# Splitting streamed weights in halves of 1024 columns instead of quarters of 512

## The chip, the cores and the metric

The kernel runs on one core of a Trainium2 chip. The metric is the device time of one launch in microseconds, the median of several runs. An execution that the hardware profiler recorded gives the trace. TensorE (PE in the rows; PEld is its weight load) does the matmuls, VectorE (DVE) and ScalarE (ACT) work elementwise, SyncE (SP) issues the DMAs.

## What is computed

The reference is a decoder of two layers over one sequence of 256 tokens with 1024 channels, all in float32. Cut to what matters:

```
for each layer:
  h = modulate(rmsnorm(x), shift1, scale1)       # shift, scale, gate = silu(c) @ wada + bada
  p = h @ win                                    # one projection, 7200 columns, split in
      # A: latent attention (q rank 768, kv rank 256, rotary key 32), wuq, wkpe, wukv expand them
      # B: stick-breaking attention, 8 heads of 64
      # C: MoBA attention, 8 heads of 64, rope on a part of the head
      # three gates of 1024 columns (sigmoid)
  m = sum over A, B, C of sigmoid(gate) * (branch @ wo)
  x = x + gate1 * (m @ wout)
  h = modulate(rmsnorm(x), shift2, scale2)
  x = x + gate2 * (relu(h @ wff1)**2 @ wff2)
x = rmsnorm(x) * g
```

## The kernel before

The weights are streamed. A **job** is one weight tile `ws` of 128 partitions and up to 2048 float32 columns (1 MB), brought by a DMA on SP's queue (L154), three buffers deep. TensorE multiplies in a rounded format (fp32r), so a weight is split in a high part `wh` = round(`ws`), written by ScalarE (L177), and a low part `wl` = `ws` - `wh`, written by VectorE (L178); activations are split likewise (`split`, L233 to L235: `lh`, `ll` and so on). Each product is then three matmuls, `wh` by the high activation, `wh` by the low one, `wl` by the high one: `mm3` (L341 to L344), and L939 to L942 for the second feed-forward matrix. `wh` and `wl` have three buffers each.

The split of a job is cut into four pieces (`PIECES`), quarters of its columns: 512 for most jobs, 384 for the six of `wuq`, 256 for the two of `wkpe`. `run(i)` emits the matmul parts of job i and spreads over them the pieces of the jobs up to two further (`AHEAD`); `pump` between the parts runs generators of attention work. After the last piece of a job the DMA of a later one is issued (`fetch_to`). Beside these there are **raw** jobs: the matrix `wada` isn't multiplied on TensorE; VectorE multiplies and sums it in two halves of 1024 columns per job (`ada`, L242, then L247).

The prologue (L988 to L1081) is written in a fixed order (`manual_schedule`); its jobs carry a list of sources (several small DMAs), four of them are not split at all (`plain`), the other four in quarters. Elsewhere the compiler's scheduler orders each engine's instructions by its own estimate, from the order in the code and the dependencies. Each engine then executes its list in order.

Steps that the text behind speaks of:
- `sb_attn` (L488 to L517), stick-breaking attention: scores `z`, then on ScalarE abs, exp, ln (L497 to L499), on VectorE L500, the split in `lh` (L234) and `ll` (L235), matmuls `z` (L510) with these, exp to `a`, and `po` (L469).
- `rope` (L574 to L586): `raw` (ScalarE, L576, recorded at the helper's line L234) and `rl` (VectorE, L235) from a product in PSUM, a product with the cosine (L579), matmuls `rp` (L582, L583), a product with the sine (L585).
- `sigmoid` (L130 to L135): abs, exp, ln on ScalarE, L134 on VectorE, exp on ScalarE; used for the branch gates.
- `mla_v` (L747): matmuls `mvps` from `wukv`, in PSUM; `pt` (L560) are transpositions of softmax tiles; `s` (L521, L524) are the scores of latent attention, of `km` and `qm`; `qm` is written by copies on VectorE (L771).

Names of small tiles in rows can be those of a tile that shares the buffer (`csr` for a constant, `head` for another).

Of the kernel before, what the change touches and what calls it, by code (L numbers as in the profile page):

```python
# [11 lines left out]
F32 = mybir.dt.float32  # L12
# [3 lines left out]
AF = mybir.ActivationFunctionType  # L16
# [24 lines left out]
def trunk(ctx, tc, xT, heads, pos, signs, masks, gfin, wada, win, wkpe, wuq, wukv, wo, wout, wff1, wff2, out):  # L41
    nc = tc.nc
# [115 lines left out]
    def fetch_to(i):  # L158
        while state["dma"] <= min(i, len(jobs) - 1):
            for _ in fetch(state["dma"]):  # L160
                pass
            state["dma"] += 1

    def split_piece():
        i, pc = divmod(state["split"], PIECES)
        job = jobs[i]
        if job.raw:
            job.parts[pc](job.ws)
        elif job.plain:
            job.wh, job.wl = job.ws, None  # L170
        else:
            if pc == 0:
                job.wh = wpool.tile([128, 2048], F32R, name="wh", tag="wh", bufs=WB)
                job.wl = wpool.tile([128, 2048], F32R, name="wl", tag="wl", bufs=WB)
            n = job.f // PIECES
            a = slice(pc * n, pc * n + n)
            nc.scalar.activation(job.wh[:, a], job.ws[:, a], AF.Copy)  # L177
            nc.vector.tensor_sub(job.wl[:, a], job.ws[:, a], job.wh[:, a].bitcast(F32))  # L178
        state["split"] += 1
        if state["auto"] and pc == PIECES - 1:  # L180
            fetch_to(i + WS)

    def split_to(i, pc):
        while state["split"] < min(PIECES * i + pc, PIECES * len(jobs)):
            split_piece()
# [994 lines left out]
```

## Time and profile before

| | us |
|---|---|
| median of 3 runs | 937.77 (935.73 to 939.75) |
| profiled execution | 938.25 |
| its span | 936.5 |
| TensorE busy | 915.7 (98%) |
| VectorE busy | 730.5 (78%) |
| ScalarE busy | 599.1 (64%) |
| mean granted TensorE clock | 0.995 of full speed |

The span runs from the first to the last recorded instruction; the rest of the time lies around it. In rows of a timeline the first number is the start in us, the second the duration, "x7" means seven in a row, and the bracket at the end is the time that the engine was idle before, with what ended the wait. The duration of a matmul is longer than its distance to the next, since matmuls are pipelined.

### The profile page before, as it was taken

To read this page: it belongs to the slowest core of one execution; us is meant where nothing else is said; L and a number is where in the kernel's file an instruction comes from. 1 tells how busy PE (TensorE), PEld (TensorE's weight loads), DVE (VectorE), ACT (ScalarE), POOL (GpSimd) and SP (SyncE) were. 2 spreads that over 40 slices of the span, in tenths; PEclk is the share of its full clock that TensorE was granted. 3 is DMA by queue.
4 is the path that set the end of the run, shared out by engine and by line. 5 is a ranking of instruction groups with operands and counts; after the bars stand their busy time and mean duration, and the time that the engine had idled before them with its cause. 6 is when DMAs were issued, how large, how long until landed. Compare 5 with 4: busy or idle time off the path is not lost.

```text
span 936.5 us, 19142 instructions
## 1 busy us (share of the span) xinstructions
PE 915.7 (98%) x7771; PEld 889.6 (95%) x7772; DVE 730.5 (78%) x1414; ACT 599.1 (64%) x1251; POOL 9.6 (1%) x15
## 2 busy tenths in 40 slices
PE   7998999999999999999999999999999999999996
PEld 4998999899999999999999999989999999999995
DVE  6878788887799976767897978879787989554554
ACT  4277678867576874645576677886677677563641
POOL 0000000000000000000000000000000000000012
PEclk9999999999999999999999999999999999999998
DMA  9956564565657388677847554645666647755531
GB/s 339 386 205 231 185 225 159 214 235 196 245 225 270 140 310 305 236 270 266 324 174 274 222 203 155 229 169 210 240 221 228 212 150 284 256 181 190 186 121 45
DMA packets 32634, 208.77 MB, mean 223 GB/s; under 512 B 3745, under 2 KB 4130, under 8 KB 8994
## 3 DMA queue, kind: packets, MB, share of 16 engines
q1 hardware_dynamic: 32400, 207.35, 61.7%
q8 instruction: 61, 1.00, 0.4%
q0 software_dynamic: 144, 0.20, 0.1%
q14 instruction: 27, 0.22, 0.1%
q10 hardware_dynamic: 2, 0.00, 0.0%
HBM read 206.49 MB, written 1.05 MB: 222 GB/s over the span
## 4 chain that ended last, share of the span: by engine, by line
PE 84%; DVE 6%; DMA 6%; ACT 2%; issue 1%; SPq 0%; DVEq 0%; ACTq 0%
PE ps L342 17%; PE ps L343 16%; PE ps L344 16%; PE ff L939 5%; PE ff L942 5%; PE ff L940 5%; DMA ws<-win 5%; PE pre L364 4%; DVE wl L178 3%; PE po L469 1%; DMA ws<-wada 1%; PE vps L342 1%; PE vps L344 1%; PE vps L343 1%; PE s L524 1%; PE z L510 1%
## 5 line engine op out<-in xcount | busy, mean ns | idle before, releaser
L178 DVE TENSOR_TENSOR wl<-ws,wh 128x512 fp32r<-128x512 f32 (+1 forms) x592 | 378.7, 675 | 128.6 <-ACT wh L177 128.0
L177 ACT ACTIVATE wh<-ws 128x512 fp32r<-128x512 f32 (+1 forms) x592 | 336.8, 615 | 208.2 <-PE ps L343 97.3
L342 PE MATMUL ps<-act,wh 128*128 128x256 f32 x1120 | 312.0, 279 | 0.0
L344 PE MATMUL ps<-act,wl 128*128 128x256 f32 x1120 | 310.3, 277 | 0.0
L343 PE MATMUL ps<-act,wh 128*128 128x256 f32 x1120 | 310.1, 277 | 0.0
L342 PEld LDWEIGHTS ps<-act,wh 128*128 128x128 f32 x1120 | 210.4, 188 | 0.5 <-DVE wl L178 0.3
L344 PEld LDWEIGHTS ps<-act,wl 128*128 128x128 f32 x1120 | 210.9, 188 | 0.0
L343 PEld LDWEIGHTS ps<-act,wh 128*128 128x128 f32 x1120 | 210.4, 188 | 0.2
L939 PE MATMUL ff<-fh,wh 128*128 128x256 f32 x448 | 123.6, 276 | 0.0
L940 PE MATMUL ff<-fl,wh 128*128 128x256 f32 x448 | 123.6, 276 | 0.0
L942 PE MATMUL ff<-fh,wl 128*128 128x256 f32 x448 | 123.6, 276 | 0.0
L242 DVE SCALAR_TENSOR_TENSOR ws<-ws,cb 128x1024 f32<-128x1024 f32 x80 | 95.9, 1221 | 22.5 <-DMA ws<-wada 22.1
L939 PEld LDWEIGHTS ff<-fh,wh 128*128 128x128 f32 x448 | 84.1, 188 | 0.0
L940 PEld LDWEIGHTS ff<-fl,wh 128*128 128x128 f32 x448 | 84.1, 188 | 0.0
L942 PEld LDWEIGHTS ff<-fh,wl 128*128 128x128 f32 x448 | 84.1, 188 | 0.0
L544 ACT ACTIVATE e<-s,st 128x128 f32<-128x128 f32 (+1 forms) x64 | 26.0, 432 | 23.6 <-DVE st L539 23.6
L364 PE MATMUL pre<-xh,wh 128*128 128x258 f32 x96 | 28.3, 295 | 0.0
L364 PE MATMUL pre<-xh,wl 128*128 128x258 f32 x96 | 27.1, 283 | 0.0
L364 PE MATMUL pre<-xl,wh 128*128 128x258 f32 x96 | 27.1, 282 | 0.0
L342 PE MATMUL vps<-wh,act 128*128 128x256 f32 x96 | 26.9, 280 | 0.0
L343 PE MATMUL vps<-wl,act 128*128 128x256 f32 x96 | 26.7, 278 | 0.0
L344 PE MATMUL vps<-wh,act 128*128 128x256 f32 x96 | 26.7, 278 | 0.0
(259 smaller groups left out, 1738.6 us busy)
## 6 DMA issues: line engine op xcount, KB each, us to landing
ws<-wff SPq DMA_DIRECT2D x64, 1024.0 KB, 4.9
ws<-win SPq DMA_DIRECT2D x50, 1024.0 KB, 4.9
ws<-wada SPq DMA_DIRECT2D x40, 1024.0 KB, 4.9
ws<-wo SPq DMA_DIRECT2D x12, 1024.0 KB, 4.9
adaw<-wada SPq DMA_DIRECT2D x8, 1024.0 KB, 9.2
ws<-wout SPq DMA_DIRECT2D x8, 1024.0 KB, 4.9
ws<-win SPq DMA_DIRECT2D x24, 256.0 KB, 9.1
ws<-wuq SPq DMA_DIRECT2D x6, 768.0 KB, 4.3
```

Of the source, the lines that this page charges most:

```text
L177: nc.scalar.activation(job.wh[:, a], job.ws[:, a], AF.Copy)
L178: nc.vector.tensor_sub(job.wl[:, a], job.ws[:, a], job.wh[:, a].bitcast(F32))
L242: nc.vector.scalar_tensor_tensor(w, w, 1.0, cb, op0=OP.mult, op1=OP.mult, accum_out=mods[l][:, 2 * b + i:2 * b + i + 1])
L342: nc.tensor.matmul(o, wh, ah, start=first, stop=False)
L343: nc.tensor.matmul(o, wh, al, start=False, stop=False)
L344: nc.tensor.matmul(o, wl, ah, start=False, stop=last)
L364: nc.tensor.matmul(ps[:, i, 0:258], w[:, c:c + 128], a[:, k, :], start=k == 0 and n == 0, stop=k == KT - 1 and n == 2, skip_group_check=True)
L469: nc.tensor.matmul(po[64 * h:64 * h + 64, u, o:256], v[:, k, vc:vc + 64], pT[:, h, c:c + n], start=k == 0, stop=k == 1, tile_position=(0, ...
L544: nc.scalar.activation(e[:, h, a:b], s[:, h, a:b], AF.Exp, scale=scale, bias=st[:, 4 + c:5 + c], accum_out=st[:, 8 + c:9 + c])
L939: nc.tensor.matmul(o, wh[:, c0:c0 + 128], fh[:, k, :], start=st, stop=False, skip_group_check=True)
L940: nc.tensor.matmul(o, wh[:, c0:c0 + 128], fl[:, k, :], start=False, stop=False, skip_group_check=True)
L942: nc.tensor.matmul(o, wl[:, c0:c0 + 128], fh[:, k, :], start=False, stop=en, skip_group_check=True)
```

## The change

The piece counter stays as it is: four pieces per job, spread over the parts as before. But where a job's source is one matrix (not a list, so outside of the prologue), piece 0 now splits the first half of the columns at once, piece 2 the second half, and pieces 1 and 3 emit nothing. The halves have 1024 columns, 768 for `wuq` and 512 for `wkpe`.

```diff
             n = job.f // PIECES
-            a = slice(pc * n, pc * n + n)
-            nc.scalar.activation(job.wh[:, a], job.ws[:, a], AF.Copy)
-            nc.vector.tensor_sub(job.wl[:, a], job.ws[:, a], job.wh[:, a].bitcast(F32))
+            wide = 1 if isinstance(job.src, list) else 2
+            if pc % wide == 0:
+                a = slice(pc * n, (pc + wide) * n)
+                nc.scalar.activation(job.wh[:, a], job.ws[:, a], AF.Copy)
+                nc.vector.tensor_sub(job.wl[:, a], job.ws[:, a], job.wh[:, a].bitcast(F32))
```

Line numbers behind L178 are higher by 2 in the changed kernel. The order on SP and POOL is the same. On TensorE the same matmuls stand in nearly the same order; ScalarE and VectorE have fewer instructions, which the scheduler has placed anew.

VectorE, the first rope and the first stick-breaking block of layer 1 (about 65 to 78 us), before:

```order
L178 TENSOR_TENSOR wl<-ws,wh 128x512 x7
L247 TENSOR_TENSOR mod_90<-mod_90,head 128x2
L500 SCALAR_TENSOR_TENSOR l<-z,l 128x768
L235 TENSOR_TENSOR ll<-l,lh 128x768
L235 TENSOR_TENSOR rl<-ps,raw 128x512
L579 TENSOR_TENSOR mbqk<-ps,tab 128x512
L500 SCALAR_TENSOR_TENSOR l<-z,l 128x768
L178 TENSOR_TENSOR wl<-ws,wh 128x512 x3
L235 TENSOR_TENSOR ll<-l,lh 128x768
```

and now:

```order
L244 SCALAR_TENSOR_TENSOR ws,mod_90<-ws,cb 128x1024
L180 TENSOR_TENSOR wl<-ws,wh 128x1024 x3
L249 TENSOR_TENSOR mod_90<-mod_90,head 128x2
L502 SCALAR_TENSOR_TENSOR l<-z,l 128x768
L237 TENSOR_TENSOR ll<-l,lh 128x768
L180 TENSOR_TENSOR wl<-ws,wh 128x1024
L502 SCALAR_TENSOR_TENSOR l<-z,l 128x768
L237 TENSOR_TENSOR rl<-ps,raw 128x512
L581 TENSOR_TENSOR mbqk<-ps,tab 128x512
L237 TENSOR_TENSOR ll<-l,lh 128x768
```

A half of `wl` and the second `l` now stand ahead of `rl` and of the product with the cosine; before they stood behind it.

ScalarE at the same place, before:

```order
L498 ACTIVATE l<-l 128x768
L234 ACTIVATE raw<-ps 128x512
L499 ACTIVATE l<-l 128x768
L177 ACTIVATE wh<-ws 128x512 x4
L234 ACTIVATE lh<-l 128x768
```

and now:

```order
L500 ACTIVATE l<-l 128x768
L179 ACTIVATE wh<-ws 128x1024
L501 ACTIVATE l<-l 128x768
L236 ACTIVATE raw<-ps 128x512
L179 ACTIVATE wh<-ws 128x1024
L236 ACTIVATE lh<-l 128x768
```

`raw` has moved behind a half of `wh` and behind the logarithm of the second block.

VectorE ahead of the gate for which `mvps` waits in layer 1 (about 163 to 169 us), before:

```order
L235 TENSOR_TENSOR latl<-lt,lath 128x256 x2
L178 TENSOR_TENSOR wl<-ws,wh 128x384
L661 SCALAR_TENSOR_TENSOR lt<-lat,head,rr 128x256 x2
L178 TENSOR_TENSOR wl<-ws,wh 128x384 x2
L242 SCALAR_TENSOR_TENSOR ws,mod_90<-ws,cb 128x1024
L134 SCALAR_TENSOR_TENSOR gate<-ps,gate 128x512
```

and now:

```order
L237 TENSOR_TENSOR latl<-lt,lath 128x256
L180 TENSOR_TENSOR wl<-ws,wh 128x768
L663 SCALAR_TENSOR_TENSOR lt<-lat,head,rr 128x256 x2
L134 SCALAR_TENSOR_TENSOR gate<-ps,gate 128x512
```

The half of `ada` (L242, now L244) that stood directly ahead of the gate has gone to an earlier place; one of 768 columns stands there for three of 384.

## Rows read from the trace of the kernel before

**Rows 1.** The page, busy time of each engine: us, share, instructions.

```profile
PE 915.7 (98%) x7771; PEld 889.6 (95%) x7772; DVE 730.5 (78%) x1414; ACT 599.1 (64%) x1251; POOL 9.6 (1%) x15
```

**Rows 2.** Stretches: length, busy PE, PEld, DVE, ACT, POOL; granted clock, DMA share, GB/s.

```profile
400.00:425.00 25.00, 25.00 (x223) 25.00 (x222) 16.40 (x30) 13.66 (x27) 0.00 (x0) 1.00 0.77 277
...
617.00:623.00 6.00, 5.04 (x18) 4.10 (x19) 3.82 (x10) 4.79 (x12) 0.00 (x0) 0.72 0.55 186
```

**Rows 3.** Waits of TensorE: us in total, times, longest.

```profile
PE mvps L342 <- DVE gate L134: 4.3, 2, 2.2
...
PE rp L582 <- ACT wh L177: 1.0, 1, 1.0
PE z L510 <- DVE ll L235: 0.9, 1, 0.9
PE po L469 <- ACT wh L177: 0.6, 1, 0.6
...
PE s L521 <- DVE qm L771: 0.2, 1, 0.2
```

**Rows 4.** Groups by line and form: busy us, mean ns of one, idle before.

```profile
L178 DVE TENSOR_TENSOR wl<-ws,wh 128x512 fp32r<-128x512 f32 x552 | 360.2, 687 | 118.2 <-ACT wh L177 117.6
L177 ACT ACTIVATE wh<-ws 128x512 fp32r<-128x512 f32 x552 | 319.7, 625 | 203.9 <-PE ps L343 93.0 <-PE ff L940 46.3 <-PE xl L940 16.2
...
L242 DVE SCALAR_TENSOR_TENSOR ws<-ws,cb 128x1024 f32<-128x1024 f32 x80 | 95.9, 1221 | 22.5 <-DMA ws<-wada 22.1
...
L178 DVE TENSOR_TENSOR wl<-ws,wh 128x384 fp32r<-128x384 f32 x24 | 12.5, 554 | 6.5 <-ACT wh L177 6.5
L177 ACT ACTIVATE wh<-ws 128x384 fp32r<-128x384 f32 x24 | 11.4, 521 | 0.0
```

**Rows 5.** Timeline of VectorE, 65 to 78 us.

```profile
65.07 4.30 DVE L178 TENSOR_TENSOR wl<-ws,wh 128x512 fp32r<-128x512 f32 x7
...
69.36 0.95 DVE L500 SCALAR_TENSOR_TENSOR l<-z,l 128x768 f32<-128x768 f32 x1
...
73.29 0.69 DVE L235 TENSOR_TENSOR rl<-ps,raw 128x512 fp32r<-128x512 f32 x1 [1.11 <-ACT raw L234]
73.90 0.68 DVE L579 TENSOR_TENSOR mbqk<-ps,tab 128x512 f32<-128x512 f32 x1
...
77.16 0.95 DVE L235 TENSOR_TENSOR ll<-l,lh 128x768 fp32r<-128x768 f32 x1
```

**Rows 6.** Timeline of ScalarE, 72 to 76 us.

```profile
72.68 0.58 ACT L234 ACTIVATE raw<-ps 128x512 fp32r<-128x512 f32 x1
73.16 0.83 ACT L499 ACTIVATE l<-l 128x768 f32<-128x768 f32 x1
73.89 2.18 ACT L177 ACTIVATE wh<-ws 128x512 fp32r<-128x512 f32 x4
```

**Rows 7.** Timeline of TensorE, 73 to 79 us.

```profile
74.68 0.47 PE L582 MATMUL rp<-raw,csr 128*128 128x512 f32 x1 [1.02 <-ACT wh L177]
...
76.20 0.27 PE L510 MATMUL z<-ll,negs 128*128 128x128 f32 x1
...
78.17 0.44 PE L510 MATMUL z<-ll,csr 128*128 128x384 f32 x1 [0.87 <-DVE ll L235]
...
79.20 0.33 PE L342 MATMUL ps<-act,wh 128*128 128x256 f32 x1
```

**Rows 8.** Timeline of TensorE at the first `po`.

```profile
88.71 0.65 PE L469 MATMUL po<-a,v 128*64 128x256 f32 x4 [0.64 <-ACT wh L177]
```

**Rows 9.** Timeline of TensorE at `mvps`, layers 1 and 2.

```profile
169.31 0.47 PE L342 MATMUL mvps<-wh,lath 128*128 128x512 f32 x1 [2.20 <-DVE gate L134]
...
172.29 0.37 PE L342 MATMUL ps<-lath,wh 128*128 128x256 f32 x1
...
617.96 0.47 PE L342 MATMUL mvps<-wh,lath 128*128 128x512 f32 x1 [2.06 <-DVE gate L134]
...
622.28 0.56 PE L342 MATMUL ps<-lath,wh 128*128 128x256 f32 x1
```

## The prediction

> **What bounds the kernel now.** I read the busy shares first. TensorE is busy 915.7 us of a span of 936.5 us, VectorE 730.5 and ScalarE 599.1 us [rows 1]. So one engine fills the span, and the two that the change relieves are 78% and 64% busy. Next the table by stretch: in the feed-forward stretch from 400 to 425 us TensorE is busy for all 25.00 us at a granted clock of 1.00, 223 matmuls, which makes 112 ns each, while VectorE has work for 16.40 us and ScalarE for 13.66 us [rows 2]. There TensorE waits for nobody, and nothing that makes a split cheaper can shorten it.
>
> What is left for the change to win stands in the list of TensorE's waits [rows 3]: the two `mvps` matmuls that wait for VectorE's gate (4.3 us together), the first rope matmul `rp` (1.0), a `z` matmul that waits for `ll` (0.9), the first `po` (0.6) and a score `s` (0.2). The waits of the prologue are not in it, since its jobs keep their quarters. That is 7.0 us in all, 0.7% of the run.
>
> **The change: fewer, longer instructions.** The rows by form hold 552 + 24 splits at 512 and 384 columns on each of the two engines [rows 4], and 16 more at 256. The prologue keeps 16 of these 592 quarters; the other 576 become 288 halves, so 288 instructions go from each engine. What one saves follows from two sizes. On VectorE 512 columns take 687 ns and 384 take 554 [rows 4]: 133 ns for 128 columns, so 1024 should take 687 + 4 x 133 = 1219 ns; the 1024-column instruction that the kernel already has on VectorE, L242, takes 1221 [rows 4]. Neighbours overlap a little: seven splits took 4.30 us [rows 5], so one starts (4.30 - 0.69)/6 = 0.602 us after the other, 0.085 less than its duration. A half then occupies about 1.22 - 0.085 = 1.13 us against 1.204 for two quarters: 0.07 us saved. On ScalarE 512 take 625 ns and 384 take 521 [rows 4], so 1024 about 625 + 4 x 104 = 1041 ns; four took 2.18 us [rows 6], a distance of 0.52, so a half occupies about 0.94 us against 1.04: 0.10 us saved. Bounds for a half are no better than one quarter (0.60, 0.52) and no worse than two full durations (1.37, 1.25); I take the extrapolations, since L242 lies on the first. Over 288 halves that is 20 us of VectorE and 29 us of ScalarE.
>
> None of it is on the path by itself: in rows 2 both engines have a third of their time free. The cover is TensorE's queue of weights: with three buffers and a lead of two jobs a weight is split long before it is multiplied. If that cover were gone, the gain would be up to the waits of rows 3.
>
> The Trainium skill bears on this ("Perfetto Trace Analysis", section "Optimizing Scalar/DVE Operations"): larger operations help where the engine is saturated, and where Scalar or Vector aren't saturated but cause bubbles on other engines, breaking instructions up lets work complete sooner. By that rule the change goes the wrong way here and the time would come out above 937.8. The trace agrees with the rule's premise (rows 1 and 3: not saturated, small bubbles); it gives no price, and none of it enters the sum.
>
> **The change: what now stands in front of others.** Each engine takes its instructions in order, so what is queued behind a split now waits for up to another half: about 0.4 us more on ScalarE, 0.53 on VectorE. The issue order of the DMAs on SP's queue and the order on POOL's are the same. TensorE's order differs at six places, each a few neighbours. I walked every wait of TensorE with the new orders and these durations.
>
> Place A, the first rope of layer 1, 56 to 90 us. Before, ScalarE writes `raw` from 72.68, then L499, then four quarters from 73.89 [rows 6]; VectorE does `rl` at 73.29, the product L579 at 73.90 until 74.58 [rows 5], and `rp` starts behind it at 74.68 [rows 7]. In the new order one half of `wh` stands before L499, and `raw` behind both: 72.68 + 0.94 + 0.73 (the distance from L499 to what follows) = 74.35, and 0.2 later still, since one half of an ada job has moved between splits and delays the first L500 (before at 69.36 [rows 5]) a little. On VectorE a half of `wl` and the second L500 come ahead of `rl`: the half waits for its `wh` until about 73.9, ends near 75.1, then L500 0.87, `rl` 0.61 and L579 0.68. L579 ends at about 77.25 and `rp` starts at 77.35 instead of 74.68: 2.67 later. But much of this comes back. The second `z` block behind it waited for its `ll`, which started at 77.16 [rows 5], and so began its second matmul only at 78.17 [rows 7]. In the new order `lh` and `ll` are done at about 76.9 and 78.1, and TensorE gets there at 78.98 (`rp` and the first `z` block took 1.63 before: the last matmul of that block starts at 76.20 [rows 7], one matmul is 0.11). Nothing is waited for any more. From the second matmul of the block to the weight matmul behind it pass 79.20 - 78.17 = 1.03 [rows 7], about 0.15 more from the first, so that weight matmul starts at 80.16 instead of 79.20: +0.97. The same order comes once more before the first `po` (88.71 [rows 8]), where I get 89.75, which makes **+1.04 for the whole of A**. Its bounds: if ScalarE's halves cost two full quarters and nothing came back, 2.67 + 0.6 = +3.3; if the scheduler's rows meet earlier than I walked, no more than the waits there are lost, 1.0 + 0.9 + 0.6 = -2.5.
>
> Place B and its twin in layer 2, `mvps` at 169.31 and 617.96 [rows 9]. The gate's chain runs over both engines (abs, exp, ln on ScalarE, L134 on VectorE). In the new order one transposition `pt` has moved behind the wait, and the ada half that stood just ahead of L134 now stands earlier, with a half of 768 columns and two short steps in its place. An ada half is 1.22 us [rows 4], that half about 0.95 (687 + 2 x 133 ns), and its `wh` on ScalarE comes later by a quarter; I let them cancel, so the wait stays and the `pt` adds one matmul of 0.11 us, half of it hidden: **+0.05 each**. Bounds: the wait goes (-2.2 each [rows 3]), or grows by one half on each engine (+0.94).
>
> The scores `s` [rows 3] wait for copies that now stand behind a half of `wl`: **+0.2 each** in two layers, between -0.2 and +0.53. In the feed-forward stretches, the output products and the rest, the steps between a weight's split and its use have over 1 us to spare: 0, cover being the lead of two jobs.
>
> Sum: 1.04 + 2 x 0.05 + 2 x 0.2 = +1.5 us. The profiled execution took 938.25 us, 0.48 above the median of 937.77; 938.25 + 1.5 - 0.48 = 939.3 us for a median.
>
> **The clock.** It is a bound that the trace shows once. After `mvps` in layer 2 the granted clock fell: 0.72 in the stretch from 617 to 623 us [rows 2]; from the first `mvps` to the first `ps` it took 622.28 - 617.96 = 4.32 us, in layer 1, after a wait of the same length, 172.29 - 169.31 = 2.98 [rows 9]. Such a fall costs 1.34 us. Place A gets one idle stretch of 3.7 us where it had three short ones, and layer 1 may fall too. So the terms reach from -1.34 (the one in layer 2 goes) to +2.68.
>
> **The rivals.** First, *faster*: the freed time shortens the waits. The chains at A and `mvps` contain splits, and VectorE has less to do ahead of them. For it: 0.07 and 0.10 us per half, and an ada half less in front of the gate. Against it: a chain passes two or three halves at most, 0.3 us, and each half can block for longer than that. Its best is all of 7.0 us and the clock's 1.34: 937.8 - 8.3 = 929.4; half of it, 933.6, is no longer 0.5%.
>
> Second, *slower*: the doubled granularity bites at all attention steps. Place: the 12 ropes, the 8 blocks of `z` and the 24 gates, whose chains change engine two to four times and can meet a half on each. Price: 0.4 + 0.53 = 0.9 us per chain that TensorE waits for. Now TensorE waits at six places in all [rows 3]. If six more lose their spare microsecond, 6 x 0.9 = 5.4 us, and with the sum above 944.7 us. It decides where the chain's end has less than about 0.9 us before TensorE; in the walk the ropes and blocks behind place A have 1.5 us or more, which speaks against it. What speaks for it is that place A alone already loses 2.67 us at one step.
>
> Third, *nothing moves*: TensorE's wait at A is as in the trace and the chip hands out the same clock; 937.8. That the change doesn't do what it says is excluded: the orders have 288 splits fewer.
>
> **How the numbers follow.** Forecast, +0.5 to +3 us (938.3 to 940.8): 0.55. Nothing or a small gain, down to -4: 0.22, of which the most lies near 937.8. A loss from +3 to +4.7 (A at its bound, a clock fall): 0.12. Slower rival, over +4.7: 0.07. Faster rival, under -4.7: 0.04. A measurement of this kernel can tell about 0.5%, 4.7 us, from no change; all but the two rivals lie within it. The range leaves out the two rivals and the outer half of the small gains: 935.5 to 942.5.
>
> **What would show it.** Splits at 1024 columns of 1.22 us on VectorE and 1.04 on ScalarE, busy sums (of durations) down by 288 x (1.37 - 1.22) = 43 and 288 x (1.25 - 1.04) = 60 us. TensorE busy as before. `rp` preceded by one wait of over 3 us and no wait left in the `z` block behind it; the `mvps` waits at 2 to 2.4 us. I would be wrong on the mechanism if `mvps` waits fell under 1 us (the faster rival), or if new waits on `wl`, `raw` or `ll` appeared behind 100 us (the slower one).

## Result and profile after

The changed kernel takes 943.85 us (938.24 to 947.26, 17 runs) against 938.0 (933.92 to 942.85, 17 runs): a ratio of 1.0053, 95% interval 1.0036 to 1.0070. It is slower by 5 to 6 us; forecast were 939.3 and a range to 942.5. Its first profiled execution, 938.24 us, is the fastest of the 17 and does not contain the loss, so the same kernel was profiled three times more (`after_b`, `after_c`, `after_d` below).

The page of that first execution, the busy times (compare [rows 1]):

```profile
PE 917.0 (98%) x7771; PEld 890.5 (95%) x7772; DVE 709.8 (76%) x1126; ACT 576.6 (62%) x963; POOL 9.8 (1%) x15
```

288 instructions less on each engine, and 20.7 and 22.5 us less busy. The groups by line and form (busy us, mean ns of one, idle before), to be held against [rows 4]:

```profile
L180 DVE TENSOR_TENSOR wl<-ws,wh 128x1024 fp32r<-128x1024 f32 x272 | 327.8, 1222 | 135.0 <-ACT wh L179 132.7 <-PE ps L345 1.6
L179 ACT ACTIVATE wh<-ws 128x1024 fp32r<-128x1024 f32 x272 | 282.1, 1056 | 196.8 <-PE ps L345 95.0 <-PE ff L942 47.4 <-DMA ws<-wff 26.1
L180 DVE TENSOR_TENSOR wl<-ws,wh 128x768 fp32r<-128x768 f32 x12 | 11.3, 952 | 9.1 <-ACT wh L179 9.1
```

The extrapolated 1219, 1041 and 953 ns became 1222, 1056 and 952. (The busy sums fell by less than the sum of durations, since neighbours that overlap count once: the 20 and 29 us that the prediction had for occupied time are nearer than its 43 and 60.) TensorE's waits in the same execution (compare [rows 3]):

```profile
PE mvps L344 <- DVE gate L134: 2.6, 2, 1.4
PE s L523 <- DVE qm L773: 2.0, 2, 1.1
...
PE rp L584 <- ACT lh L236: 0.6, 1, 0.6
```

`mvps` waits less than in [rows 3], `s` much more.

### The profile page after: what moved, and what is told of

The parts are those of the page before. It is cut to its first block, busy times and chain, and to the rows that moved or that the text cites. A ratio compares the mean times of both kernels' runs of the same rounds, so it can differ in the third digit from the quotient of the medians.

```text
span 936.5 us, 18563 instructions
## 1 busy us (share of the span) xinstructions
PE 917.0 (98%) x7771; PEld 890.5 (95%) x7772; DVE 709.8 (76%) x1126; ACT 576.6 (62%) x963; POOL 9.8 (1%) x15
## 4 chain that ended last, share of the span: by engine, by line
PE 72%; DVE 10%; DMA 10%; ACT 5%; issue 2%; SPq 0%; DVEq 0%; ACTq 0%
PE ps L344 15%; PE ps L345 15%; PE ps L346 14%; DMA ws<-win 5%; DVE wl L180 4%; PE ff L942 4%; PE ff L941 4%; PE ff L944 4%; DMA ws<-wada 4%; PE pre L366 4%; DVE ws L244 2%; ACT wh L179 2%; PE po L471 1%; PE vps L344 1%; PE vps L346 1%
## 5 line engine op out<-in xcount | busy, mean ns | idle before, releaser
L180 DVE TENSOR_TENSOR wl<-ws,wh 128x1024 fp32r<-128x1024 f32 (+3 forms) x304 | 349.4, 1169 | 148.4 <-ACT wh L179 145.9
L179 ACT ACTIVATE wh<-ws 128x1024 fp32r<-128x1024 f32 (+3 forms) x304 | 301.2, 1013 | 207.5 <-PE ps L345 99.6
L244 DVE SCALAR_TENSOR_TENSOR ws<-ws,cb 128x1024 f32<-128x1024 f32 x80 | 96.2, 1219 | 28.8 <-DMA ws<-wada 28.8
```

What stands on the lines that cost most here:

```text
L244: nc.vector.scalar_tensor_tensor(w, w, 1.0, cb, op0=OP.mult, op1=OP.mult, accum_out=mods[l][:, 2 * b + i:2 * b + i + 1])
```

## The experiments

All ratios are to the kernel before on the same chip, with 95% intervals.

**Once more, and where.** `after_b` is the changed kernel again, `before_b` the one before. `halves_ff` and `halves_rest` split the change by a flag on the job:

```diff
-            wide = 1 if isinstance(job.src, list) else 2
+            wide = 2 if job.ff else 1                                        # halves_ff
+            wide = 1 if job.ff or isinstance(job.src, list) else 2           # halves_rest
```

> The changed kernel once more, for another profiled execution: the one at hand took 938.24 us, its median is 943.85, so it does not contain the 5.5 us. Theory C (clock): about 944 us, the granted clock near 0.991 instead of 0.996, with two to four stretches at a lower clock that the first profile lacks, TensorE's waits behind 56 us about 6 us in all as there. Theory W (waits, my slower rival): about 944 us at a clock near 0.995, with 5 us more of waits behind 56 us, on halves of wl, raw, ll or on a DMA of weights. Theory P (prologue): the 5 us stand before 56 us.

> The kernel before once more, for a second profiled execution. All theories: 938 +- 3 us. Theory C: clock 0.994 or higher, the lower stretch behind mvps in layer 2 there or not. Theory W and P: the same waits as in the first profile, to 1 us.

> Halves of 1024 only in the feed-forward jobs (64 of 148), quarters elsewhere. Theory W: the feed-forward has over 4 us between a split and its use, so 938.0, ratio 1.000. Theory C: the clock could also fall there, since longer splits load the engines in another pattern; ratio between 1.000 and 1.003. Theory P: ratio 1.000.

> Halves everywhere outside of the prologue but in the feed-forward jobs, which keep quarters. Theory W: all of the loss, ratio 1.005 to 1.006 (943). Theory C: between 1.002 and 1.006, at a clock that is lower than before's. Theory P: ratio 1.005.

`after_b`: 944.58 us, 1.0059 (1.0039 to 1.0080). `before_b`: 939.61. `halves_ff`: 937.68, 0.9989 (0.9966 to 1.0012). `halves_rest`: 942.88, 1.0044 (1.0025 to 1.0063). The feed-forward's halves cost nothing and bring nothing; the loss lies in the other stretches. The mean granted clock of the runs is 0.9928 in `after_b` and 0.9938 in the 29 runs of before beside it; theory C alone would need more than that 0.001, about 1 us (in `wuq_fix` below the difference is 0.0021, about 2 us).

**By stretch.** The same halves in one part of the jobs at a time (`wide = 2 if 8 <= i < 20 else 1` and so on; layer 2 by `i >= 100 and not job.ff`).

> Halves only in the jobs 8 to 19, the first projections of layer 1 with place A (60 to 110 us); quarters everywhere else. My prediction's walk: +1.0 us there (939.3, ratio 1.001). Theory A (most of the loss sits at place A in executions whose first ada transfer lands later than in the profiled one): ratio 1.003 to 1.004. Theory S (the loss is spread over many small waits): ratio 1.001.

> Halves only in the jobs 20 to 34 (latents, mvps, the scores s of layer 1, 115 to 195 us). The traces of the changed kernel show 1 to 1.5 us of wait at s and 0.6 less at mvps: theory S +1 us, ratio 1.001; theory A 1.0005.

> Halves only in the jobs 35 to 57 (branch C, the gates and the output product of layer 1, 195 to 300 us). The traces show 0.5 to 0.9 us of waits on the merged activation at 275 to 295 us: theory S +0.7 us, ratio 1.001; theory A 1.000.

> Halves only in layer 2 outside of the feed-forward (480 to 750 us), where place A has no twin, since layer 2 has no first rope behind a prologue. Theory S: half of the loss, +2.5 us, ratio 1.0025. Theory A: +0.5 to 1 us (s and the output product), ratio 1.001.

`halves_early` 939.37, 1.0019 (1.0003 to 1.0036); `halves_mid` 938.6, 1.0009 (0.9988 to 1.0031); `halves_late` 938.3, 0.9997 (0.9977 to 1.0016); `halves_l2` 939.28, 1.0022 (1.0002 to 1.0041). Together 0.0047, as much as `halves_rest`: the parts add up, though each is known to about 0.002 only. The medians speak for theory S: theory A had 1.003 to 1.004 for the first and 1.001 for layer 2. The intervals still hold 1.003 and 1.001, so theory A isn't excluded. My walk had +0.25 us for all of layer 2, where 2 us are lost (0.2 to 3.8 by the interval).

**Dose, and which engine.** `whole` sets `wide = 4`; in `halves_act` only the ScalarE line is under `if pc % wide == 0`, in `halves_dve` only the VectorE line (at the second piece of a half). `s_fix` is the changed kernel with quarters in four jobs (`i in (33, 34, 134, 135)`).

> The changed kernel, but with quarters in the four jobs (33, 34 and their twins in layer 2) whose low parts stand ahead of the copies that the scores s wait for; VectorE's order there is then again a quarter, the sum, the ada half, the copies. Over ten traces the stretch around s is 0.65 us longer with halves in layer 1 and 1.64 in layer 2. Theory S (many small waits, of which these are the largest two): the waits at s fall from 2 to 3 us to under 0.5, and 2.3 us of the 5.5 go, 941.5, ratio 1.003. Theory R (the loss is not in these waits; it would come back elsewhere): 943.5, ratio 1.005 or more.

> Each job outside of the prologue is split in one instruction of 2048 columns per engine. Theory S: what stands in front of others grows from one extra quarter to three, so the loss grows to about three times 5.5, 954 us, ratio 1.012 to 1.02. If the loss came from fewer instructions as such or from the clock and not from what they block: 943 to 945, ratio 1.005 to 1.008.

> Halves on ScalarE only, VectorE keeps its quarters. VectorE is the fuller engine (78%), and the copies ahead of s are its own. If VectorE's blocking is the loss: ratio 1.000 to 1.001. If a half of the high part hurts because the low part and raw wait for it: 1.002 to 1.004.

> Halves on VectorE only, ScalarE keeps its quarters. If VectorE's blocking is the loss: ratio 1.003 to 1.005. If ScalarE's is: 1.001 or less.

`whole`: 957.93, 1.0212 (1.0189 to 1.0236), 3.6 times the loss of `after_b`, while the instructions saved are 1.5 times as many (432 for 288). So the loss grows with what a longer split holds up, and with the order that comes with it (below), not with the number of instructions. The waits of TensorE in `whole`:

```profile
PE mvps L344 <- ACT km L736: 5.6, 2, 2.8
PE rp L584 <- ACT lh L236: 4.7, 1, 4.7
...
PE ps L346 <- DVE wl L180: 3.0, 3, 1.5
```

`halves_act`: 942.99, 1.0054 (1.0033 to 1.0075); `halves_dve`: 941.28, 1.0042 (1.0017 to 1.0067). Either engine alone loses nearly what both lose, so the loss belongs to neither of them alone. I take it that the chains that TensorE waits for alternate between the engines, and that a half on either holds the chain up; no run shows this by itself.

A rival is left in all of these runs. Whenever the splits change, the scheduler also moves instructions that are no splits: compared with the kernel before, 75 of 822 on VectorE and 27 of 659 on ScalarE have another place among themselves in the changed kernel, 81 and 34 in `whole`. No run keeps the order and changes the length alone, so a longer split and a worse order are not told apart.

`s_fix`: 942.62, 1.0052 (1.0035 to 1.0070): mending `s` alone does not show in the time, as theory R had it, although the order there is restored. Its trace shows what was not mended, VectorE first, then TensorE:

```profile
633.75 1.23 DVE L244 SCALAR_TENSOR_TENSOR ws<-ws,cb 128x1024 f32<-128x1024 f32 x1 [0.83 <-DMA ws<-wada]
...
639.77 1.24 DVE L773 COPY qm<-t 32x256 f32<-32x256 f32 x4
```

```profile
640.11 0.81 PE L523 MATMUL s<-km,qm 96*128 96x128 f32 x4 [0.98 <-DVE qm L773]
```

`s` starts 6.36 us behind the ada half, as with quarters, but VectorE stood 0.83 us ahead of that half for its transfer, and TensorE still waits 0.98.

**Place A, both places, smaller pieces.** `a_fix` has quarters for all jobs below 20, `as_fix` also for 28 to 36 and 129 to 137; `eighths` splits every piece outside of the prologue in two instructions.

> The changed kernel with quarters in the jobs up to 19, so that both engines' order at place A is that of before. The traces: with the new order rp starts 14.7 us behind the start of the first ada half instead of 11.9 (2.80 later, the walk had 2.67), and in two traces the one long idle stretch there is followed by a fall of the granted clock (0.50 from 78 to 80 us), with which the matmuls behind it end 1.36 us later. At the same arrival of the ada weight, place A then loses 2.3 us. If that is typical of the timed executions: 941.5, ratio 1.003, mean clock up by about 0.0015 to 0.994. If the loss is elsewhere: 943.5, ratio 1.005.

> As a_fix, and quarters too in the jobs around mvps and the scores s of both layers (28 to 36 and 129 to 137 without the raw ones). Spread theory: both largest places are mended; left are about 1.5 us at the output products and the seam of the layers: 939.5 to 940.5, ratio 1.002. If it is more, the rest sits in waits that the traces don't show.

> The other direction: outside of the prologue each quarter is split in two instructions, of 256 columns for most jobs. VectorE gets about 288 x 0.14 = 39 us more to do (420 ns each, 0.085 overlapped), ScalarE 46 us, both still under 85%. If what counts is what a split blocks: 936 to 938, ratio 0.998 to 1.000. If what counts is that the order of the pieces moves at all, or the engines' load: 940 to 943, ratio 1.002 to 1.005.

> The changed kernel a third time, for one more profiled execution. Its time should be between 940 and 946. If the prologue keeps its clock (first matmul behind it near 50 us), rp should start 14.7 us behind the first ada half, with a fall of the clock behind it; if the prologue is late (53.5), rp should be bound by TensorE, and place A cost nothing.

`a_fix`: 941.65, 1.0019 (0.9999 to 1.0040). `as_fix`: 939.65, 1.0007 (0.9985 to 1.0029). `after_c`: 946.64. So quarters in the nine jobs around the first rope take back half of the loss or more (halves in these jobs alone, `halves_early`, cost a third of it), and those around `mvps` and `s` most of what is left, while five sixths of the jobs keep their halves. That last step, from `a_fix` to `as_fix`, is 2 us, and the intervals overlap; in the one trace of `as_fix` TensorE still waits at `s` in layer 2:

```profile
PE s L523 <- DVE qm L773: 1.4, 1, 1.4
```

There VectorE stood 1.50 us for an ada transfer that was issued as early as with quarters throughout, but took 6.9 us to land.

`eighths`: 942.44, 1.0044 (1.0017 to 1.0070): pieces of 256 lose too. That is against theory S, and is the other branch of its expectation: that the order moves at all (61 instructions of 822 on VectorE and 20 of 659 on ScalarE), or the load. In its one trace TensorE waits 1.1 us for `mh` at the output product, which it did in neither execution before (the 0.8 for `ml` stands in `before_b` too), and the stretch there, 202 to 306 us, takes 106.3 us against 104.0 to 105.5 with quarters. What makes `mh` late is open.

**Whose transfer.** In `after_c` the wait at `s` in layer 2 begins with an ada transfer that comes late. `wuq_fix` has quarters in the six `wuq` jobs alone (`job.f == 1536`).

> The changed kernel with quarters (of 384) in the six jobs of wuq alone. The order at the scores s keeps its halves, so s should still start 8.03 us behind the start of the ada half before it (6.67 with quarters). What changes is when the ring gives its buffer to that ada transfer: its issue waits for the last wl of the wuq job three before it, and in layer 2 comes 1.5 us later, against TensorE, with halves of 768; VectorE then stands 1.7 to 2.9 us ahead of the ada half. Theory D (the late transfer is a good part of the loss at s): that idle time falls under 0.5 us, s in layer 2 comes 1 to 1.5 us earlier against TensorE, time 941 to 942.5, ratio 1.003 to 1.0045. Theory B (only the longer order behind it counts): idle as before, ratio 1.005 to 1.006.

> The changed kernel a fourth time: one more profiled execution for the table by stretch. 940 to 946 us; s - ada 8.03 in layer 2 and 1.4 to 3 us of idle time on VectorE ahead of the ada half; a fall of the clock behind s where TensorE's gap is near 2 us or longer.

`wuq_fix`: 944.42, 1.0069 (1.0046 to 1.0091); `after_d`: 941.26. The forecast of theory D failed: with quarters there VectorE stood not shorter but longer ahead of the ada half, VectorE and TensorE of `wuq_fix`:

```profile
635.87 1.23 DVE L244 SCALAR_TENSOR_TENSOR ws<-ws,cb 128x1024 f32<-128x1024 f32 x1 [3.33 <-DMA ws<-wada]
```

```profile
643.89 1.08 PE L523 MATMUL s<-km,qm 96*128 96x128 f32 x4 [2.14 <-DVE qm L773]
```

The issue of the transfers shows what stayed. On SP's queue in `before_b`, then in the first execution after, then in `wuq_fix` (start, length of the pair, "x2" two issues):

```profile
621.34 2.48 SPq L154 DMA_DIRECT2D ws<-wo  x2
627.14 0.33 SPq L154 DMA_DIRECT2D ws<-wada  x1
```

```profile
615.83 7.16 SPq L154 DMA_DIRECT2D ws<-wo  x2
626.15 0.33 SPq L154 DMA_DIRECT2D ws<-wada  x1
```

```profile
618.93 6.53 SPq L154 DMA_DIRECT2D ws<-wo  x2
628.78 0.33 SPq L154 DMA_DIRECT2D ws<-wada  x1
```

The two `wo` transfers ahead of the ada one were issued 2.2 us apart before and are 6.2 to 6.8 apart now; the ada transfer follows the second one by 3.5 us (3.65 in `wuq_fix` and in `before_b`). Counted from the same weight matmul near 631 us, most of this is the first one, which goes out 2.8 to 3.4 us earlier than in `before_b`: there it goes out with the ada sum (L247 at 621.35), now right behind a split of `wl`. The second goes out 1.2 to 1.7 us later and the ada transfer 1.1 to 1.6 later, each 0.03 us behind the end of a split of `wl`. The quarters in `wuq` did not bring the ada issue forward (1.2 us later than in `before_b`), so this run does not decide how much of the loss the late transfer is.

## Why the prediction was wrong

**Where the time goes.** The starts of the same matmul can be compared between traces. From six to ten executions with halves in a stretch and six to eight without, of all the kernels above, the mean difference of each stretch, in us:

```
stretch (us, before)                     predicted   measured
place A, to 94                             +1.0        +1.0
mvps layer 1, 151 to 185                   +0.05       +0.4   (clock falls in both kernels)
s layer 1, 185 to 202                      +0.2        +0.5
rest of layer 1, 202 to 306                 0          +0.3
feed-forward with the seam at 475           0          +0.5
layer 2 to 637, with mvps                  +0.05       -0.9
s layer 2, 637 to 655                      +0.2        +2.8
rest                                        0           0.0
sum                                        +1.5        +4.6
```

Single stretches of single executions vary by 1 to 5 us, mostly by the clock, so most terms of 0.5 are not to be told from nothing. In `s` of layer 2 the two groups lie apart: 18.7 to 24.5 us with halves, 17.6 to 18.1 with quarters. The sum agrees with the timed loss of 5 to 6 within that.

**Place A: the walk was right, but left the clock's fall to the range.** `rp` was to start at 77.35 with the ada half at 62.77, 14.58 behind it (11.91 before). In six traces of halves it is 14.69 to 14.70; in two others TensorE itself came later. `after_d` is the clearest, VectorE:

```profile
61.97 1.23 DVE L244 SCALAR_TENSOR_TENSOR ws<-ws,cb 128x1024 f32<-128x1024 f32 x1 [6.34 <-DMA ws<-wada]
...
73.27 1.23 DVE L180 TENSOR_TENSOR wl<-ws,wh 128x1024 fp32r<-128x1024 f32 x1 [1.56 <-ACT wh L179]
74.41 0.95 DVE L502 SCALAR_TENSOR_TENSOR l<-z,l 128x768 f32<-128x768 f32 x1
75.28 0.68 DVE L237 TENSOR_TENSOR rl<-ps,raw 128x512 fp32r<-128x512 f32 x1
75.88 0.68 DVE L581 TENSOR_TENSOR mbqk<-ps,tab 128x512 f32<-128x512 f32 x1
```

TensorE, and behind it the table by stretch (length, busy PE, PEld, DVE, ACT, POOL, granted clock, DMA share, GB/s):

```profile
76.66 0.77 PE L584 MATMUL rp<-raw,csr 128*128 128x512 f32 x1 [3.12 <-ACT lh L236]
...
81.81 0.52 PE L344 MATMUL ps<-act,wh 128*128 128x256 f32 x1
```

```profile
74.00:76.00 2.00, 0.00 (x0) 0.00 (x0) 2.00 (x4) 2.00 (x3) 0.00 (x0) 1.00 0.37 156
76.00:78.00 2.00, 1.34 (x4) 1.18 (x5) 2.00 (x3) 2.00 (x4) 0.00 (x0) 0.50 0.00 0
78.00:80.00 2.00, 2.00 (x9) 2.00 (x8) 2.00 (x3) 0.70 (x2) 0.00 (x0) 0.50 0.27 45
```

The half of `wl`, then `l`, then `rl` and L581, as walked; one long wait, none in the `z` block behind it, as forecast. (It was over 3 us, as forecast, in this one of the eight executions alone.) The delay is one of order as much as of length: of the 2.8 us, 75.28 - 74.41 = 0.87 is the `l` that now stands ahead of `rl`. But with the clock at 0.50 (1.2 instead of 2.4 GHz) from `rp` to the weight matmul pass 81.81 - 76.66 = 5.15 us where the walk had 2.81: the fall that I kept as a bound of the range came in three of eight executions, those in which TensorE stood longest at `rp` (2.1, 2.1 and 3.1 us in the list of waits; 1.2 or less in the others). Where TensorE arrives later, the wait is shorter: a fall of the clock in the prologue (below) delays TensorE, while the ada transfer sets the time of `rp`. That is why single executions reach from a gain, as in the first one profiled, to +3. That their mean is the +1.0 of the forecast is luck, since the forecast had neither the late TensorE nor the fall in its sum.

**The scores `s` in layer 2: the step that failed.** I gave +0.2, with a bound of +0.53, from half a microsecond of a longer split ahead of the copies. Before, from the ada half to `s`, VectorE and TensorE:

```profile
632.44 1.22 DVE L242 SCALAR_TENSOR_TENSOR ws<-ws,cb 128x1024 f32<-128x1024 f32 x1
...
634.50 1.28 DVE L178 TENSOR_TENSOR wl<-ws,wh 128x512 fp32r<-128x512 f32 x2
...
636.31 0.68 DVE L178 TENSOR_TENSOR wl<-ws,wh 128x512 fp32r<-128x512 f32 x1
...
638.77 2.45 DVE L771 COPY qm<-t 32x256 f32<-32x256 f32 x8
```

```profile
639.11 0.81 PE L521 MATMUL s<-km,qm 96*128 96x128 f32 x4 [0.16 <-DVE qm L771]
```

and in `after_c`:

```profile
637.34 1.23 DVE L244 SCALAR_TENSOR_TENSOR ws<-ws,cb 128x1024 f32<-128x1024 f32 x1 [2.90 <-DMA ws<-wada]
...
638.50 1.22 DVE L180 TENSOR_TENSOR wl<-ws,wh 128x1024 fp32r<-128x1024 f32 x1
...
640.23 1.22 DVE L180 TENSOR_TENSOR wl<-ws,wh 128x1024 fp32r<-128x1024 f32 x1
...
643.78 1.22 DVE L180 TENSOR_TENSOR wl<-ws,wh 128x1024 fp32r<-128x1024 f32 x1
645.03 2.15 DVE L773 COPY qm<-t 32x256 f32<-32x256 f32 x7
```

```profile
645.37 1.23 PE L523 MATMUL s<-km,qm 96*128 96x128 f32 x4 [1.91 <-DVE qm L773]
```

```profile
645.00:647.00 2.00, 1.63 (x6) 1.54 (x7) 1.82 (x7) 0.00 (x0) 0.00 (x0) 0.60 0.95 283
647.00:649.00 2.00, 2.00 (x9) 1.73 (x8) 1.96 (x4) 0.00 (x0) 0.00 (x0) 0.50 0.79 328
```

Three things add up, of which I had a part of the first. The steps from the ada half to `s` take 8.03 us instead of 6.67, since three halves stand among them where three quarters stood. Ahead of it VectorE stands idle for its transfer, 1.7 to 3.3 us in the eight executions with halves there, under 0.3 in those with quarters throughout; I had taken the order of the DMAs into account, not when they are issued, although each issue waits for a split. The idle time is longest where the transfer was also slow: from issue to landing it took 6.2 us in `after_c` and 7.0 in `wuq_fix`, 5.1 to 5.3 in the six others. And where the wait at `s` is longest the clock falls (1.5 to 2.1 us in `after_c`, `a_fix`, `halves_l2` and `wuq_fix`; 1.1 to 1.5 and no fall in the four others); the stretch is then 2.9 to 6.6 us longer than with quarters, against 0.8 to 1.5 without a fall.

So the term that failed is the +0.2 for `s`: it priced a part of one longer split, left out when the transfer comes, and left the clock's fall to the range; the traces show +2.8 in layer 2. How much of the timed 5 to 6 us hangs on it is not shown. `halves_l2` loses 2 us, but neither `s_fix` nor `wuq_fix`, which were to mend this step, is faster than the changed kernel, and in the one trace of `as_fix`, which is, the wait at `s` is still there.

The rival that I gave 0.07, longer splits that bite in the chains of the attention steps, comes nearest to what happened, but at one step and its clock rather than at six, and its sign, new waits on `wl`, `raw` or `ll` behind 100 us, did not appear in the four executions after. That its price of 944.7 lies near the measured time is luck.

**`mvps`.** Forecast were waits of 2 to 2.4 us as before; after, the first execution has

```profile
167.52 0.50 PE L344 MATMUL mvps<-wh,lath 128*128 128x512 f32 x1 [1.39 <-DVE gate L134]
...
617.22 0.50 PE L344 MATMUL mvps<-wh,lath 128*128 128x512 f32 x1 [1.22 <-DVE gate L134]
```

That is 0.8 us of wait each less than [rows 9], but the second execution of the kernel before has less as well:

```profile
PE mvps L342 <- DVE gate L134: 3.0, 2, 1.6
```

Over all executions with halves or quarters on both engines the wait is 1.2 to 2.4 us with halves and 1.5 to 2.2 with quarters in layer 1, no difference to be told; in layer 2 it is 1.2 to 1.4 against 1.4 to 2.9. There the ada half that left its place ahead of the gate seems to be worth more than the halves cost; I had let the two cancel. The -0.9 of the table comes from two of the six executions with quarters, `before` and `halves_late`, in which the clock fell there; it fell in none of the nine with halves.

**The rest held.** In time the feed-forward pays nothing; in the traces the seam behind it takes 15.0 to 16.7 us with halves in the feed-forward and 15.0 to 15.3 with quarters, a term that I had at 0. The freed time did not shorten the waits (the faster rival): those of TensorE between 56 and 912 us (over 0.15 us each) sum to 5.8, 7.1, 8.6 and 8.6 us in the four executions after, and to 7.3 and 6.9 in the two before. The Trainium skill says that, where Scalar or Vector aren't saturated but cause bubbles on other engines, breaking instructions up may let work be completed sooner ("Perfetto Trace Analysis", "Optimizing Scalar/DVE Operations"). Read in reverse, this has the sign of the result; below the quarters the times do not follow it (`eighths`).

What is not settled: why `s_fix` alone moves the time so little while `as_fix` beyond `a_fix` takes 2 us (the intervals overlap), what the new order does without longer splits, and why the transfer's time to land varies.

## What to carry to other kernels

Where one engine is the bound and others feed it, cutting a feeder's instructions in fewer pieces frees time that nobody waits for and can lengthen every chain that has a piece in its queue; look for the two or three chains with a bubble, and keep the pieces there as they were. Smaller pieces are no cure by themselves: here they lost too. When instructions are merged, follow the DMAs too, and not only their order: a split that ended later issued a transfer 1.1 to 1.6 us later here, and an engine that waits for it at the head of its queue holds up everything behind. A wait is not only its own length: put the clock's fall behind it into the sum when it grows to the length of one that the trace shows with a fall.

## What the hardware showed beyond that

After the same wait the clock can fall or not. In the prologue TensorE waits the same 3.1 us in both kernels; the stretch behind it, before and in the first execution after:

```profile
22.00:24.00 2.00, 2.00 (x11) 1.77 (x10) 1.89 (x6) 1.97 (x4) 0.00 (x0) 1.00 1.09 385
```

```profile
22.00:24.00 2.00, 2.00 (x6) 1.55 (x6) 2.00 (x5) 1.97 (x4) 0.00 (x0) 0.50 1.07 389
```

It fell in 13 of the 20 traces, with the same prologue, and where it fell the prologue took some 1 to 3 us longer, of which place A gives much back. Such falls are a good part of the 9 us by which single executions of one kernel differ: `after_c` took 8.4 us more than the first execution after, and 2.5 and 4.2 us of it lie in the two stretches (151 to 185 and 637 to 655 us) in which its clock fell. The first execution had no fall behind the prologue, which is a part of how it could hide the loss.
